# Down projection of the second block's FFN: the first group of hidden rows is loaded by token halves, between two weight blocks, and staged in tiles of its own

## The chip, the cores and the metric

The kernel runs on one core of a Trainium2 chip. The metric is the device time of one execution in microseconds (us). The trace was taken by the hardware profiler from one execution; the engines in it are TensorE (PE), VectorE (DVE), ScalarE (ACT), GpSimd (POOL) and SyncE (SP, which here only issues DMAs).

## The reference, cut to what matters

Two blocks run one after the other on 1024 tokens of width 1024. Each has two layers. The change is in the second half of each layer of the second block, a gated FFN with a short causal convolution; D_FF is 2816, which is 22 rows of 128.

```python
def conv_ffn(h, w_up, conv_w, conv_b, w_down):
    up = h @ w_up
    s_len = up.shape[1]
    padded = jnp.pad(up, ((0, 0), (CONV_WIDTH_2 - 1, 0), (0, 0)))
    conv = conv_b + padded[:, 0:s_len] * conv_w[0]
    for j in range(1, CONV_WIDTH_2):
        conv = conv + padded[:, j:j + s_len] * conv_w[j]
    gate, val = jnp.split(conv, 2, axis=-1)
    return (jax.nn.silu(gate) * val) @ w_down

def second_block(...):
    for l in range(DEPTH):
        ...
        x = x + conv_ffn(rms_norm(x, norm2_g[l]), w_up[l], conv_w[l], conv_b[l], w_down[l])
    return rms_norm(x, final_g)
```

## The kernel before

Every product is made of three matmuls on numbers that are split into a high and a low part (`mm3`): hi times hi (L226), lo times hi (L227) and hi times lo (L228), 128x128 by 128x512 each. So each operand is first split: ACT casts it to the high part (L214 for weights, L1358 for activations), and DVE subtracts that from the raw values (L201, in `split_lo`; in the FFN's up products one in six goes to POOL, L199).

`ffn` works in two parts. First come the 22 hidden rows. For each row `q` TensorE makes seven half-size products (`p12`, `p65`, `p7`, `p43`, a Strassen-like scheme), DVE adds them up (L1490, L1497, L1505 to L1507, L1512, L1515), `conv` runs the convolution (ACT L1463, then DVE L1465 twice for each side), `hidden` gates it (ACT L346, DVE L347, DVE L1471), and SP stores the row to DRAM (L1472, `hid_d`). Each row's tiles are two y tiles, `cv` and `fth`.

Then comes the down product. The 22 rows go through it in five groups, `[(0, 4), (4, 9), (9, 13), (13, 18), (18, 22)]`. `load_h(gi, j)` loads row `j` back, both token halves (`key` 0 and 1, 128x512 each, 256 KB), and splits them. `down(gi, m, ...)` loads weight block `m` of the group (`load_w`, L213) and makes the products of both halves; the first group's products are added to the residual, which is loaded for it (L1573, L1574), and the later groups' are added to that sum (L1570). After block `m >= 2` (`DS`) of a group one row of the next group is loaded.

All these loads, of hidden rows and of weights alike, land in the pool `wr`, which has three 256 KB buffers (tiles named `wraw`); a buffer is free again when ACT's cast and DVE's subtraction have read it. The split weights are in `wt` (four blocks), the split rows in the pools `left` (groups 0 to 3) and `dz` (group 4 alone, 16 tiles for hi and 16 for lo). `dz` takes its room from tiles of the FFN's activations and weights, so its first use waits for products that read those.

A scheduler orders the instructions of each engine from the order in the code, the buffers and its estimates of when each can run. Each engine and SP's queue then work through their own list strictly in order: where an instruction waits, all behind it on that list wait too.

Of the kernel before, what the change touches and what calls it, by code (L numbers as in the profile page):

```python
# [9 lines left out]
F32 = mybir.dt.float32  # L10
# [31 lines left out]
DS = 2  # L42
# [23 lines left out]
def run(steps):  # L66
    for _ in steps:
        pass
# [21 lines left out]
class Net:  # L90
# [1323 lines left out]
    def ffn(self, l, B, xd, finish):  # L1414

        nc, tc, I = self.nc, self.tc, self.I
        NJ = 22
        self.lo_pool = LP_FFN
        with self.right(f"fw{l}", 2) as fw, self.right(f"fe{l}", 2) as fe, self.right(f"ft{l}", 2) as ft:
# [3 lines left out]
            o, b = COLS["cw"][0] + 132 * l + 66, COLS["cb"][0] + 44 * l + 22  # L1423
# [52 lines left out]
            def mul(*ab):  # L1476

                ps = self.bank(self.all_banks)
                for i, ((hi, lo), b) in enumerate(ab):
                    for k in range(4):  # L1480
                        c = slice(k * 128, k * 128 + 128)
                        self.mm3(ps, hi[:, c], lo[:, c], B[b][k][0], B[b][k][1], i == 0 and k == 0, i == len(ab) - 1 and k == 3)
                return ps
# [36 lines left out]
            for q in range(HEAD):  # L1520
                (a11, a12), (a21, a22) = [[tuple(x[:, o:o + 512] for x in self.pre[2 * q + i]) for o in (0, 512)]
                                          for i in range(2)]
                ps = mul((a11, "11")), mul((a12, "21")), mul((a21, "11")), mul((a22, "21"))
# [17 lines left out]
        groups = [(0, 4), (4, 9), (9, 13), (13, 18), (18, 22)]  # L1541
        with ExitStack() as es:
            left = [es.enter_context(tc.tile_pool(name=f"hd{l}{i}", bufs=16 + 4 * i, reuse_waits="tile")) for i in range(2)]
            es3 = ExitStack()
            es3.enter_context(self.norm_scratch(f"f{l}"))
            xp, dz = [es3.enter_context(self.right(f"{n}{l}", 16)) for n in ("fx", "hz")]
            X = [[None] * 8 for key in range(2)]
            hid = {}

            def load_h(gi, j):  # L1550
                pool = dz if gi == 4 else left[gi % 2]
                for key in range(2):
                    raw = self.wr.tile([128, 512], F32, name="wraw", tag="wraw")
                    nc.sync.dma_start(out=raw, in_=self.hid_d[j, :, key * 512:key * 512 + 512])
                    hid[j, key] = self.split(pool, raw)

            def down(gi, m, keys, then):
                a, b = groups[gi]
                self.gemm_fm(I["w_down"][l, m][:, a:b], [(key, [hid[j, key] for j in range(a, b)], 512) for key in keys],
                             then, nk=b - a)  # L1560

            for j in range(*groups[0]):
                load_h(0, j)
            self.banks = self.all_banks
            for gi in range(4):
                nxt = list(range(*groups[gi + 1]))
                for m in range(8):
                    def ev(key, ps, n, gi=gi, m=m):
                        if gi:
                            nc.vector.tensor_add(X[key][m], ps, X[key][m])  # L1570
                            return
                        x = X[key][m] = xp.tile([128, 512], F32, name="fxn")
                        nc.sync.dma_start(out=x, in_=xd[m, :, key * 512:key * 512 + 512])  # L1573
                        nc.vector.tensor_add(x, ps, x)  # L1574

                    down(gi, m, [0, 1], ev)
                    if nxt and m >= DS:
                        load_h(gi + 1, nxt.pop(0))
            es.close()
            self.open_h(False)  # L1580
            self.banks = [(self.psA, "mm")]
            acc = [self.nm.tile([128, 512], F32, name="nacc", bufs=2) for key in range(2)]

            def last(key, m):
                def ev(key, ps, n):
                    x = X[key][m]
                    nc.vector.tensor_add(x, ps, x)
                    if l == 0:
                        nc.sync.dma_start(out=xd[m, :, key * 512:key * 512 + 512], in_=x)
                    self.sq_acc(acc[key], x, 512, m)  # L1590

                down(4, m, [key], ev)

            for m in range(8):
                last(0, m)
            self.meanwhile = lambda: [last(1, m) for m in range(MW)]
            norm = finish(0, X[0], acc[0])
            next(norm)
            for m in range(MW, 8):
                last(1, m)  # L1600
                for _ in range(NS):
                    next(norm, None)
            run(norm)
            run(finish(1, X[1], acc[1]))
            es3.close()
# [238 lines left out]
```

## Time and profile before

| | us |
|---|---|
| median of 3 runs | 3561.25 |
| lowest and highest of them | 3557.47, 3565.32 |
| the profiled execution's own time | 3559.54 |
| its span in the trace (first to last instruction) | 3557.5 |

The profiled execution has 2.0 us outside its span, and lies 1.7 us under the median. Of the span PE is busy 3420.8 us (96%), DVE 2479.8 (70%), ACT 1210.2 (34%) and POOL 628.3 (18%); the mean granted clock of TensorE is 0.984 of its full speed. The busy shares are averages over unlike stages, and what a stage is worth is read from the stage itself.

### The profile page before, as it was taken

How to read it: one execution, taken by the hardware profiler on the slowest of the kernel's cores; microseconds unless marked ns; L12 is line 12 of the kernel's file. 1: busy time of each engine (PE TensorE's matmuls, PEld its weight loads, DVE VectorE, ACT ScalarE, POOL GpSimd, SP SyncE). 2: the span in 40 equal slices, each digit the busy share in tenths (PEclk: the TensorE clock that was granted, in tenths of full speed). 3: DMA queues.
4: the chain of work that ended last, by engine and by line, in shares of the span. 5: the costliest groups of instructions: out<-in, count | busy, mean ns of one | idle time of the engine just before them, and what ended most of it. 6: DMA issues, size and time to landing. Idle time of an engine off the chain costs nothing.

```text
span 3557.5 us, 46933 instructions
## 1 busy us (share of the span) xinstructions
PE 3420.8 (96%) x17414; PEld 2725.9 (77%) x17414; DVE 2479.8 (70%) x3933; ACT 1210.2 (34%) x2189; POOL 628.3 (18%) x548
## 2 busy tenths in 40 slices
PE   7999999999989999999999998999999999999998
PEld 4888766788866687877788887887887878877786
DVE  5986578568467866454799998447355599999645
ACT  4115156331333641123344333223113243333322
POOL 4012321001033220220222320000030032222000
PEclk9999999999998999999999999999999999999999
DMA  6322365533223234316222224324324422222532
GB/s 204 87 78 83 104 183 167 174 107 97 75 87 94 82 125 140 92 46 192 78 86 83 77 80 136 117 87 150 86 60 132 144 80 77 77 78 69 174 100 92
DMA packets 245972, 380.70 MB, mean 107 GB/s; under 512 B 29104, under 2 KB 103792, under 8 KB 245232
## 3 DMA queue, kind: packets, MB, share of 16 engines
q1 hardware_dynamic: 237872, 370.37, 33.4%
q10 hardware_dynamic: 7872, 7.35, 0.8%
q8 instruction: 137, 2.24, 0.3%
q14 instruction: 91, 0.75, 0.1%
HBM read 280.35 MB, written 97.26 MB: 106 GB/s over the span
## 4 chain that ended last, share of the span: by engine, by line
PE 72%; DVE 14%; issue 5%; DMA 4%; ACT 3%; POOL 2%; SPq 0%; DVEq 0%; POOLq 0%; ACTq 0%
PE mm L226 13%; PE mm L227 13%; PE mm L228 13%; PE sc L226 4%; PE ax L226 4%; PE ax L227 3%; PE ax L228 3%; PE sc L227 3%; PE sc L228 3%; DVE wlo L201 2%; PE mm L956 2%; PE mm L942 2%; DVE cv L1465 1%; PE ax L715 1%; PE ax L1296 1%
## 5 line engine op out<-in xcount | busy, mean ns | idle before, releaser
L226 PE MATMUL mm<-hi,whi 128*128 128x512 f32 (+1 forms) x1780 | 690.8, 388 | 26.0 <-ACT whi L214 14.8
L228 PE MATMUL mm<-hi,wlo 128*128 128x512 f32 (+1 forms) x1780 | 685.9, 386 | 6.0 <-DVE wlo L201 6.0
L227 PE MATMUL mm<-lo,whi 128*128 128x512 f32 (+1 forms) x1780 | 688.0, 387 | 1.4 <-DVE lo L1651 1.1
L214 ACT CAST whi<-wraw 128x512 fp32r<-128x512 f32 (+3 forms) x412 | 232.3, 583 | 579.2 <-PE mm L227 247.8
L226 PEld LDWEIGHTS mm<-hi,whi 128*128 128x128 f32 x1780 | 337.5, 190 | 99.0 <-ACT whi L214 16.1
L228 PEld LDWEIGHTS mm<-hi,wlo 128*128 128x128 f32 x1780 | 336.8, 189 | 80.4 <-DVE wlo L201 9.4
L227 PEld LDWEIGHTS mm<-lo,whi 128*128 128x128 f32 x1780 | 337.5, 190 | 71.5 <-DVE lo L1651 3.1
L201 DVE TENSOR_TENSOR wlo<-wraw,whi 128x512 fp32r<-128x512 f32 (+3 forms) x412 | 269.4, 671 | 155.9 <-ACT whi L214 154.8
L226 PE MATMUL sc<-hi,whi 128*128 128x512 f32 x732 | 289.4, 395 | 12.5 <-ACT whi L214 10.6
L227 PE MATMUL sc<-lo,whi 128*128 128x512 f32 x732 | 288.2, 394 | 3.3 <-DVE lo L1651 3.3
L228 PE MATMUL sc<-hi,wlo 128*128 128x512 f32 x732 | 287.7, 393 | 1.6 <-DVE wlo L201 1.6
L226 PE MATMUL mm<-whi,hi 128*128 128x512 f32 (+2 forms) x704 | 259.5, 370 | 8.3 <-DVE ggt L347 8.3
L228 PE MATMUL mm<-whi,lo 128*128 128x512 f32 (+2 forms) x704 | 255.9, 364 | 0.0
L227 PE MATMUL mm<-wlo,hi 128*128 128x512 f32 (+2 forms) x704 | 255.6, 364 | 0.0
L188 POOL TENSOR_TENSOR rs<-rs,mhalf 128x4 f32<-128x4 f32 (+1 forms) x19 | 19.5, 1028 | 1072.3 <-DVE rs L183 1072.3
L498 DVE SCALAR_TENSOR_TENSOR ca<-u,wh,ca 128x1024 f32<-128x1024 f32 (+1 forms) x180 | 185.5, 1031 | 3.0
L226 PE MATMUL ax<-hi,whi 128*128 128x512 f32 x456 | 181.1, 397 | 4.8 <-DVE xn L1380 4.7
L228 PE MATMUL ax<-hi,wlo 128*128 128x512 f32 x456 | 179.8, 394 | 0.4 <-DVE wlo L201 0.4
L227 PE MATMUL ax<-lo,whi 128*128 128x512 f32 x456 | 179.9, 395 | 0.0
L201 DVE TENSOR_TENSOR wlo<-wr,whi 128x512 fp32r<-128x512 f32 x200 | 174.8, 885 | 0.0
L226 PEld LDWEIGHTS sc<-hi,whi 128*128 128x128 f32 x732 | 138.4, 189 | 43.8 <-ACT whi L214 11.2
L227 PEld LDWEIGHTS sc<-lo,whi 128*128 128x128 f32 x732 | 138.4, 189 | 35.5 <-DVE lo L1651 5.5
(367 smaller groups left out, 6568.7 us busy)
## 6 DMA issues: line engine op xcount, KB each, us to landing
wr<-in_w_up SPq DMA_DIRECT2D x80, 512.0 KB, 3.6
wraw<-in_w_fm SPq DMA_DIRECT2D x108, 256.0 KB, 3.1
wm<-in_w_mod SPq DMA_DIRECT2D x96, 256.0 KB, 3.8
wraw<-in_w_down SPq DMA_DIRECT2D x96, 256.0 KB, 2.8
hid_d<-fth SPq DMA_DIRECT2D x44, 512.0 KB, 2.6
wraw<-hid_d SPq DMA_DIRECT2D x88, 256.0 KB, 2.9
wraw<-in_w_out SPq DMA_DIRECT2D x80, 256.0 KB, 3.5
yl<-y_d SPq DMA_DIRECT2D x64, 256.0 KB, 3.3
```

What stands on the lines that cost most here:

```text
L188: nc.gpsimd.tensor_tensor(out, out, e, op=ALU.pow)
L201: nc.vector.tensor_sub(out, x, f(hi))
L214: nc.scalar.copy(hi[:, c], r)
L226: nc.tensor.matmul(ps, sh, mh, start=start, stop=False)
L227: nc.tensor.matmul(ps, sh, ml, start=False, stop=False)
L228: self.mark = nc.tensor.matmul(ps, sl, mh, start=False, stop=stop)
L498: self.not_before(nc.vector.scalar_tensor_tensor(a, u[:, j:j + n], wh[:, c, j:j + 1], a, op0=ALU.mult, op1=ALU.add))
L715: nc.tensor.matmul(o_, a_, b_, start=first_, stop=last_)
L942: nc.tensor.transpose(pt[:, j * 128:j * 128 + 128], P[:, h, kt * 128:kt * 128 + 128], self.ident)
L956: nc.tensor.matmul(po[half[u], :256], vst[:, vt, 64 * v:64 * v + 64], PT[kt][:, u * 256:u * 256 + 256], start=kt == 0, stop=kt == nkt - 1)
L1296: nc.tensor.matmul(pi[:, hv], A[h % 2][:, h // 2, :], V[:, j, hv], start=True, stop=True)
L1465: nc.vector.scalar_tensor_tensor(t[:, o:], x[:, 0:S - o], wc(2 - o), t[:, o:], op0=ALU.mult, op1=ALU.add)
```

## The change

The first group's eight half rows no longer go through `wr`: they are loaded into tiles of their own, named `hraw`, in `dz`, the place of the last group. The code's order is now: the four rows' first token half, weight block 0, the four rows' second half, weight block 1, and then all products of the group by `gemm_seq` with a lag of one, so that the second half of a weight block is multiplied one block later. Groups 1 to 3 are as before. Lines after the first group stand 16 lines lower in the changed kernel (the hidden loads are L1556 there, the residual's L1579).

```diff
--- before.py
+++ after.py
@@ -1547,10 +1547,12 @@
             X = [[None] * 8 for key in range(2)]
             hid = {}
 
-            def load_h(gi, j):
+            def load_h(gi, j, keys=(0, 1)):
                 pool = dz if gi == 4 else left[gi % 2]
-                for key in range(2):
-                    raw = self.wr.tile([128, 512], F32, name="wraw", tag="wraw")
+                for key in keys:
+
+                    raw = (self.wr.tile([128, 512], F32, name="wraw", tag="wraw") if gi else
+                           dz.tile([128, 512], F32, name="hraw", tag="h"))
                     nc.sync.dma_start(out=raw, in_=self.hid_d[j, :, key * 512:key * 512 + 512])
                     hid[j, key] = self.split(pool, raw)
 
@@ -1559,19 +1561,33 @@
                 self.gemm_fm(I["w_down"][l, m][:, a:b], [(key, [hid[j, key] for j in range(a, b)], 512) for key in keys],
                              then, nk=b - a)
 
-            for j in range(*groups[0]):
-                load_h(0, j)
+
+            a, b = groups[0]
+            wd = [I["w_down"][l, m][:, a:b] for m in range(8)]
+            early = []
+            for key in range(2):
+                for j in range(a, b):
+                    load_h(0, j, [key])
+                early.append(self.load_w(wd[key].rearrange("p k c -> p (k c)"), (b - a) * 128))
             self.banks = self.all_banks
-            for gi in range(4):
+            acts = [(key, [hid[j, key] for j in range(a, b)], 512) for key in range(2)]
+            nxt = list(range(*groups[1]))
+
+            def first_ev(m):
+                def ev(key, ps, n):
+                    x = X[key][m] = xp.tile([128, 512], F32, name="fxn")
+                    nc.sync.dma_start(out=x, in_=xd[m, :, key * 512:key * 512 + 512])
+                    nc.vector.tensor_add(x, ps, x)
+                    if key and nxt and m >= DS:
+                        load_h(1, nxt.pop(0))
+                return ev
+
+            self.gemm_seq([(wd[m], acts, first_ev(m)) for m in range(8)], 1, b - a, early)
+            for gi in range(1, 4):
                 nxt = list(range(*groups[gi + 1]))
                 for m in range(8):
-                    def ev(key, ps, n, gi=gi, m=m):
-                        if gi:
-                            nc.vector.tensor_add(X[key][m], ps, X[key][m])
-                            return
-                        x = X[key][m] = xp.tile([128, 512], F32, name="fxn")
-                        nc.sync.dma_start(out=x, in_=xd[m, :, key * 512:key * 512 + 512])
-                        nc.vector.tensor_add(x, ps, x)
+                    def ev(key, ps, n, m=m):
+                        nc.vector.tensor_add(X[key][m], ps, X[key][m])
 
                     down(gi, m, [0, 1], ev)
                     if nxt and m >= DS:
```

What the scheduler makes of it is alike in both layers; the rows below are of layer 0. In them `fth_19595` is hidden row 20, the last but one, and `fth_19740` row 21, the last.

On SP's queue, at the end of the hidden rows, before the change: the store of row 20, then half rows of group 0 (`wraw_19798` to `wraw_19810`), then the weight blocks 0 to 2, then row 4, the first row of group 1 (`wraw_19930`, `wraw_19936`). Three half rows of group 0 were loaded at the beginning of the FFN, two more stand just ahead of this piece.

```order
L1472 DMA hid_d_114<-fth_19595 128x1024
L1554 DMA wraw_19798<-hid_d_114 128x512
L1554 DMA wraw_19804<-hid_d_114 128x512
L1554 DMA wraw_19810<-hid_d_114 128x512
L213 DMA wraw_19818<-in_w_down 128x512
L213 DMA wraw_19856<-in_w_down 128x512
L213 DMA wraw_19894<-in_w_down 128x512
L1554 DMA wraw_19930<-hid_d_114 128x512
L1554 DMA wraw_19936<-hid_d_114 128x512
```

On SP's queue at the same place, after the change: `wraw_19952` to `wraw_20052` are row 4, row 5 and half of row 6 (all of group 1), `wraw_19966` and `wraw_20016` are the weight blocks 4 and 5, and the eight `hraw` are group 0, of which three are shown.

```order
L1472 DMA hid_d_114<-fth_19595 128x1024
L1556 DMA wraw_19952<-hid_d_114 128x512
L1556 DMA wraw_19958<-hid_d_114 128x512
L213 DMA wraw_19966<-in_w_down 128x512
L1556 DMA wraw_20002<-hid_d_114 128x512
L1556 DMA wraw_20008<-hid_d_114 128x512
L213 DMA wraw_20016<-in_w_down 128x512
L1472 DMA hid_d_114<-fth_19740 128x1024
L1556 DMA wraw_20052<-hid_d_114 128x512
L1556 DMA hraw_19768<-hid_d_114 128x512
L1556 DMA hraw_19774<-hid_d_114 128x512
L1556 DMA hraw_19780<-hid_d_114 128x512
```

The loads of group 1, two weight blocks and the store of the last row now stand ahead of the loads of group 0. Weight blocks 0 to 2 moved to the beginning of the FFN, where three half rows of group 0 were; block 3 stands just ahead of this piece.

On DVE, the last hidden row's end before the change (`cv_19714` and `cv_19736` are its two sides, `wlo` the weight blocks 0 to 2, `lo_19933` and `lo_19939` row 4 of group 1); the low parts of group 0 all stand ahead of this piece.

```order
L1465 SCALAR_TENSOR_TENSOR cv_19714<-y1_19683,ch_16596,cv_19714 128x1023
L1515 TENSOR_TENSOR y0_19615<-sc_19722,y0_19615 128x512
L1465 SCALAR_TENSOR_TENSOR cv_19714<-y1_19683,ch_16596,cv_19714 128x1022
L201 TENSOR_TENSOR wlo_19817<-wraw_19818,whi_19816 128x512
L1465 SCALAR_TENSOR_TENSOR cv_19736<-y0_19615,cols_82,cv_19736 128x1023
L201 TENSOR_TENSOR wlo_19855<-wraw_19856,whi_19854 128x512
L1465 SCALAR_TENSOR_TENSOR cv_19736<-y0_19615,cols_82,cv_19736 128x1022
L201 TENSOR_TENSOR wlo_19893<-wraw_19894,whi_19892 128x512
L201 TENSOR_TENSOR lo_19933<-wraw_19930,hi_19932 128x512
L347 SCALAR_TENSOR_TENSOR fth_19740<-fth_19740,cv_19736 128x1024
L201 TENSOR_TENSOR lo_19939<-wraw_19936,hi_19938 128x512
L1471 TENSOR_TENSOR fth_19740<-fth_19740,cv_19714 128x1024
```

On DVE the same place after the change, from the low part of the first `wraw` of group 1 on.

```order
L201 TENSOR_TENSOR lo_19955<-wraw_19952,hi_19954 128x512
L1465 SCALAR_TENSOR_TENSOR cv_19736<-y0_19615,cols_82,cv_19736 128x1022
L201 TENSOR_TENSOR lo_19961<-wraw_19958,hi_19960 128x512
L347 SCALAR_TENSOR_TENSOR fth_19740<-fth_19740,cv_19736 128x1024
L201 TENSOR_TENSOR lo_20005<-wraw_20002,hi_20004 128x512
L1471 TENSOR_TENSOR fth_19740<-fth_19740,cv_19714 128x1024
L201 TENSOR_TENSOR lo_20011<-wraw_20008,hi_20010 128x512
L201 TENSOR_TENSOR lo_20055<-wraw_20052,hi_20054 128x512
L201 TENSOR_TENSOR lo_19771<-hraw_19768,hi_19770 128x512
L201 TENSOR_TENSOR lo_19777<-hraw_19774,hi_19776 128x512
```

The low parts of rows 4, 5 and 6 (`lo_19955` to `lo_20055`) are interleaved with the last row's end, and the low parts of group 0 come behind it. ACT's casts stand in the same order as these low parts. On PE the first product of group 0 (`mm_19828`) takes `hi_19770`, the high part of `hraw_19768`, first.

## Rows read from the trace of the kernel before

**Rows 1.** PE's waits, 2060 to 2420 us (layer 0) and 3281 to 3490 us (layer 1); total, times, longest.

```profile
PE mm L226 <- ACT whi L214: 10.1, 1, 10.1
...
PE sc L226 <- ACT whi L214: 10.6, 1, 10.6
```

**Rows 2.** Chain that ended last, layer 0, around PE's wait; start us, us, what.

```profile
2180.07 0.70 DVE lo L201
2180.78 3.79 DMA wraw<-hid_d
...
2185.30 0.70 DVE lo L201
2186.02 2.65 DMA wraw<-in_w_down
...
2188.69 0.63 ACT whi L214
...
2189.36 0.80 PE mm L226
```

**Rows 3.** PE's timeline after each wait; start us, us, line, operation, idle before.

```profile
2194.90 0.39 PE L226 MATMUL mm<-hi,whi 128*128 128x512 f32 x1
...
3296.64 0.80 PE L226 MATMUL sc<-hi,whi 128*128 128x512 f32 x1 [10.58 <-ACT whi L214]
...
3300.63 0.39 PE L227 MATMUL sc<-lo,whi 128*128 128x512 f32 x1
```

**Rows 4.** Windows: us; PE, PEld, DVE, ACT, POOL busy; PEclk; DMA share; GB/s.

```profile
2120.00:2160.00 40.00, 40.00 (x174) 32.37 (x173) 38.23 (x43) 15.35 (x22) 10.11 (x6) 1.00 0.16 53
2189.40:2194.60 5.20, 5.20 (x12) 4.11 (x13) 4.73 (x7) 2.38 (x3) 0.00 (x0) 0.50 0.31 95
```

**Rows 5.** DVE's timeline, layer 0, end of the hidden rows.

```profile
2163.85 0.68 DVE L1497 TENSOR_TENSOR y<-mm,y 128x512 f32<-128x512 f32 x1
...
2167.76 0.69 DVE L1512 TENSOR_TENSOR y<-sc,y 128x512 f32<-128x512 f32 x1
...
2169.82 1.28 DVE L1465 SCALAR_TENSOR_TENSOR cv<-y,ch,cv 128x1023 f32<-128x1023 f32 x1 [0.78 <-ACT cv L1463]
...
2173.42 2.60 DVE L1465 SCALAR_TENSOR_TENSOR cv<-y,cols,cv 128x1023 f32<-128x1023 f32 x2
2175.93 0.68 DVE L1490 TENSOR_TENSOR y<-sc,y 128x512 f32<-128x512 f32 x1
...
2177.19 1.23 DVE L347 SCALAR_TENSOR_TENSOR fth<-fth,cv 128x1024 f32<-128x1024 f32 x1
2178.33 0.69 DVE L201 TENSOR_TENSOR lo<-wraw,hi 128x512 fp32r<-128x512 f32 x1
2178.93 1.22 DVE L1471 TENSOR_TENSOR fth<-fth,cv 128x1024 f32<-128x1024 f32 x1
...
2194.53 1.28 DVE L1465 SCALAR_TENSOR_TENSOR cv<-y,cols,cv 128x1022 f32<-128x1022 f32 x1
...
2197.19 1.23 DVE L347 SCALAR_TENSOR_TENSOR fth<-fth,cv 128x1024 f32<-128x1024 f32 x1 [0.18 <-ACT fth L346]
```

**Rows 6.** DVE's timeline, layer 1, the last but one row's end.

```profile
3281.30 0.68 DVE L1490 TENSOR_TENSOR y<-ax,y 128x512 f32<-128x512 f32 x1
3282.56 1.23 DVE L347 SCALAR_TENSOR_TENSOR fth<-fth,cv 128x1024 f32<-128x1024 f32 x1 [0.58 <-ACT fth L346]
```

**Rows 7.** SP's timeline in the FFN of layer 0; start us, us of issuing.

```profile
1788.24 0.38 SPq L1472 DMA_DIRECT2D hid_d<-fth  x1
1793.51 0.33 SPq L1554 DMA_DIRECT2D wraw<-hid_d  x1
1793.93 0.89 SPq L1442 DMA_DIRECT2D wr<-in_w_up  x1
...
2203.46 6.43 SPq L1573 DMA_DIRECT2D fxn<-x_d  x10
```

**Rows 8.** All hidden loads (L1554) of the kernel, from issue to landing.

```profile
DMA to landing us min/median/max: 2.4/2.9/6.1
```

## The prediction

> **What bounds the kernel now.** I read the list of PE's waits around the down products first, since PE is busy 96% of the span and only a wait of PE is worth anything. It has one line in each layer [rows 1]: PE stands still for 10.1 us in layer 0 and 10.6 us in layer 1, between the last product of the hidden rows and the first down product, and waits for nothing else in that stretch. So the change can win the 20.7 us of these two waits and what hangs on them, and no more; the lag of one, which is to spare later products a wait, finds none there to spare.
>
> The chain shows what makes up the wait [rows 2]. A DVE low part frees a `wr` buffer at about 2180.7, a hidden load goes out in it and takes 3.79 us, its low part frees the buffer again, weight block 0 goes out, lands after 2.65 us, is cast, and PE starts at 2189.36. Two loads stand one behind the other through three buffers, and the buffers are freed by DVE. DVE in turn is late: it is busy 38.23 of 40 us in the FFN [rows 4] and still has the last row's L347 to do at 2197.19 [rows 5], when PE has been out of hidden rows since 2189.36 - 10.1 = 2179.3. So at this place DVE is some 18 us behind PE, and whatever waits for DVE's last instructions comes late.
>
> The wait has a second price. After it the granted clock is 0.50 for a while [rows 4], which is 1.2 GHz where 1.00 is 2.4: from 2189.36 to 2194.90 in layer 0, and from 3296.64 to 3300.63 in layer 1 [rows 2, 3]. Of these 5.5 and 4.0 us about half is lost, 4.8 us in all.
>
> **What the change does to the restart.** Had the staged loads gone out as soon as their place was free, they would stand clear of the buffers. But in SP's order after the change five loads of group 1, weight blocks 4 and 5, and the store of row 21 stand ahead of them. The last, `wraw_20052`, needs the third buffer back from `lo_20011`, and on DVE `lo_20011` stands behind the last row's L1471. Before, group 0's loads needed nothing of the last row's L347 and L1471; now they stand behind both.
>
> That a wait in SP's queue holds what stands behind it is seen in the trace [rows 7]. A store went out at 1788.24, nothing for 5.3 us, then a hidden load at 1793.51, and 0.42 us behind it a load of up weights, which goes into a pool of its own. The Trainium skill, "DMA: Bandwidth & Descriptors", section "Anatomy of one DMA — SWDGE (gpsimd) path", says that any wait for a semaphore happens on the issuing sequencer, before dispatch. By that rule the staged loads wait with the group 1 load ahead of them, and the time is that of the sum below; without it they could pass, as in the rival on the other side. The row agrees, for SP's queue.
>
> **The restart in layer 0, worked out.** I start from row 21's L1490, at 2175.93 [rows 5], up to which DVE's order is the same but for which raw values a low part is taken of, and walk DVE's new order to the start of `lo_20011`. Each step is the distance of starts in a row of the same instructions:
> L1490 and a low part 1.26 (to 2177.19), row 20's L347 1.14 (to 2178.33), and L1471, of the same size, 1.14: 3.54.
> L1497 to L1512: 3.91 for the row before, which had two low parts between; now one, so less 0.60 (a low part, 2178.33 to 2178.93): 3.31.
> L1512 to L1465, with ACT's L1463 between: 2.06. From there to side 0's first L1465, one low part included: 3.60.
> That L1465, half of the 2.51 us that two take, 1.25, and `lo_19955` 0.60: 1.85.
> The second L1465 to L347, with a low part and ACT's tanh between: 2.66.
> L347 1.14, `lo_20005` 0.60, L1471 1.14: 2.88.
> The sum is 19.90, so `lo_20011` starts at 2195.83. The loads that these low parts need keep up just so: `lo_20005` stands 4.40 us behind the start of `lo_19955`, which frees its buffer, and the cycle is 0.71 to the issue, 2.9 to land [rows 8] and 0.63 of cast [rows 2], 4.24.
>
> From there: 0.71 from the low part's start to the load that takes its buffer (2180.07 to 2180.78), 0.64 to the next issue (10 loads in 6.43 us) [rows 7], 3.79 to land, 0.67 from cast to PE [rows 2]. PE starts at 2201.64 in place of 2189.36: **12.3 us later**. For the landing I take 3.79 and not the median 2.9 [rows 8], because that load, as the new one, goes out just behind a store of 512 KB.
>
> **Layer 1.** Row 21's L1490 starts at 3281.30 and L347 1.26 later [rows 6]. Here a low part stands between L347 and L1471, so the first step is 1.26 + 1.14 + 0.60 + 1.14 = 4.14, the sum 20.50, and the low part that stands where `lo_20011` does in layer 0 starts at 3301.80. With 5.81 behind it PE starts at 3307.61 and not 3296.64 [rows 3]: **11.0 us later**.
>
> **The rest of the edits, at nothing.** Weight blocks 0 to 2 are loaded at the FFN's beginning, in buffers that then held hidden rows; the loads, casts and low parts are as many as before. The staged tiles' place was last read by products that PE has long done. After the restart PE needs a new half row for each three matmuls: 3 x 0.43 = 1.3 us at the half clock (12 in 5.20) and 3 x 0.23 = 0.69 at full clock (174 in 40 us) [rows 4], and they go out 0.64 apart, so they keep up; if not, it costs under 1 us a layer. Weight block 4 is cast behind the eight half rows, 8 x 0.63 = 5 us, while PE has eight products or 96 x 0.23 = 22 us to do with the four blocks at hand. The half clock after the wait I leave as long as it was; the longer wait could change that, and as no row shows a wait of 22 us here I bound it by none and by twice what it is, 4.8 us either way.
>
> **Sum.** 12.28 + 10.97 = 23.2 us on the profiled execution's 3559.54 (a span of 3557.5 and 2.0 outside) gives 3582.8. The median of the runs shown is 1.7 higher, so 3584.5.
>
> Bounds: a landing of 2.4 or 6.1 in place of 3.79 [rows 8] gives -2.8 or +4.6 for both layers. If DVE's idle times in the walk (0.78 and 0.18, and 0.58 more in layer 1) [rows 5, 6] all vanished, -2.5. With the clock's 4.8 either way that is 3574 to 3594.
>
> **Rivals.** *The staged loads are not held* (faster). They go out when their place is free, before PE has run out, and both waits nearly vanish, with the half clock behind them: at most 20.7 + 4.8 = 25.5, less about 1 us a wait, so about 3538. For it speaks that these tiles need no buffer of `wr`; against it SP's order and [rows 7], and beyond that DVE's order, in which the low part of the first staged row, which PE's second matmul needs, also stands behind the last row's L1471. It decides where `lo_20011` starts before 2189.36 - 5.81 = 2183.5 in layer 0, 12.3 us of a walk of 19.9 earlier. Chance 0.07.
> *The restart comes when it did* (no change). The staged loads end about when the old weight load ended, because DVE is less late than the walk says. The eight low parts that no longer stand in the tail, 8 x 0.60 = 4.8 us, speak for it, but the walk leaves them out already, and it has only about 1 us of idle time in layer 0. 3561. Chance 0.06.
> *Half the loss* (slower by less). DVE catches up some 4 to 7 us a layer, for instance because ACT's tanh and convolution start come sooner with fewer casts ahead: 3567 to 3574, about 3570. Chance 0.08.
> *A longer loss.* The `wr` loads ahead land late, up to 6.1 us [rows 8]; then the cycle of 4.24 becomes 7.4, past the 4.40 that DVE leaves it, and moves `lo_20011` by up to 3 us a layer, on top of the bound above: 3589 + 6 = 3595. Chance 0.06.
>
> **How the numbers follow.** The forecast has 0.73; with the smaller and the longer loss, 0.87 lie on the slower side. A measurement of this kernel can tell about 0.2%, 7 us, from no change: faster 0.07, same 0.06, slower 0.87. The range reaches from 3570, the middle of the smaller loss, to 3595, the middle of the longer one: it leaves out the first two rivals (0.13) and about half of the other two (0.07), which is 2 in 10.
>
> **What would show it.** In the changed profile PE's wait before group 0 should be 22.4 us and 21.6 us, ended by ACT's cast of an `hraw`; the first staged load should go out near 2197.2 and 3303.2, 0.6 us behind a load of a `wraw` that waited for a DVE low part, itself right behind L1471. The later groups should show no new wait. Wrong it would be if the staged loads go out ahead of that low part, if DVE reaches L1471 of row 21 before 2190, or if the wait is longer but the half clock behind it is gone.

## The result, and the profile after

The changed kernel takes 3585.98 us in the median of 4 runs (3582.16 to 3589.82), against 3563.28 us for the kernel before in 4 runs (3557.47 to 3566.28). The ratio is 1.0068 with a 95% interval of 1.0047 to 1.0089: slower by 22.7 us, where 23.2 were forecast. The profiled execution took 3582.16 us (span 3580.4), 22.6 more than that of before.

PE's waits of the changed kernel, 2060 to 2420 us and 3281 to 3520 us, answer to [rows 1]; the columns are the total, the times and the longest. The other lines of the first list lie before the down products.

```profile
PE mm L226 <- ACT hi L1358: 22.5, 1, 22.5
...
PE sc L226 <- ACT hi L1358: 21.5, 1, 21.5
```

Each layer still has one wait, no longer ended by the cast of weight block 0 but by that of a hidden half row. It was 10.1 and 10.6 us.

SP's timeline of the changed kernel at that place shows what the half rows wait for; start, us of issuing.

```profile
2181.28 0.32 SPq L1472 DMA_DIRECT2D hid_d<-fth  x1
2182.48 3.64 SPq L1556 DMA_DIRECT2D wraw<-hid_d  x2
2190.25 0.33 SPq L213 DMA_DIRECT2D wraw<-in_w_down  x1
2192.09 2.07 SPq L1556 DMA_DIRECT2D wraw<-hid_d  x2
2196.24 0.33 SPq L213 DMA_DIRECT2D wraw<-in_w_down  x1
2197.38 0.32 SPq L1472 DMA_DIRECT2D hid_d<-fth  x1
2197.98 0.32 SPq L1556 DMA_DIRECT2D wraw<-hid_d  x1
2198.35 4.31 SPq L1556 DMA_DIRECT2D hraw<-hid_d  x8
```

PE has run out at 2203.26 - 22.47 = 2180.79. The queue gets through nine entries in the 17 us from 2181.28 on, each when DVE has freed a buffer or ended a row, and all eight staged loads follow without a gap, 0.37 us behind the last `wraw`. They show no wait of their own, so what held them was the queue's order. Whether their place held them too is taken up with the third run.

DVE's timeline of the changed kernel, the walk of the prediction from L1490 to the low part that frees the last buffer; it answers to [rows 5].

```profile
2177.50 0.69 DVE L1490 TENSOR_TENSOR y<-sc,y 128x512 f32<-128x512 f32 x1
...
2194.39 1.23 DVE L347 SCALAR_TENSOR_TENSOR fth<-fth,cv 128x1024 f32<-128x1024 f32 x1 [0.57 <-ACT fth L346]
2195.53 0.68 DVE L201 TENSOR_TENSOR lo<-wraw,hi 128x512 fp32r<-128x512 f32 x1
2196.13 1.22 DVE L1471 TENSOR_TENSOR fth<-fth,cv 128x1024 f32<-128x1024 f32 x1
2197.27 0.68 DVE L201 TENSOR_TENSOR lo<-wraw,hi 128x512 fp32r<-128x512 f32 x1
2202.57 0.69 DVE L201 TENSOR_TENSOR lo<-wraw,hi 128x512 fp32r<-128x512 f32 x1 [4.62 <-ACT hi L1358]
```

From 2177.50 to 2197.27 are 19.77 us, against the 19.90 of the walk. After it DVE itself has nothing to do for 4.6 us: with the last row done, all wait for the load.

PE's timeline of the changed kernel at the two restarts; it answers to [rows 3].

```profile
2203.26 0.80 PE L226 MATMUL mm<-hi,whi 128*128 128x512 f32 x1 [22.47 <-ACT hi L1358]
...
2206.57 0.39 PE L227 MATMUL mm<-lo,whi 128*128 128x512 f32 x1
...
3319.10 0.80 PE L226 MATMUL sc<-hi,whi 128*128 128x512 f32 x1 [21.54 <-ACT hi L1358]
...
3322.55 0.40 PE L227 MATMUL sc<-lo,whi 128*128 128x512 f32 x1
```

The matmuls are back at 0.39 to 0.40 us after 3.3 and 3.4 us, where it took 5.5 and 4.0 before. The full clock comes back a little sooner after the longer wait, worth some 1 us in layer 0.

### The profile page after: what moved, and what is told of

Same layout as the page of the kernel before. It is cut to its first block, busy times and chain, and to the rows that moved or that the text cites. A ratio compares the mean times of both kernels' runs of the same rounds, so it can differ in the third digit from the quotient of the medians.

```text
span 3580.4 us, 46898 instructions
## 1 busy us (share of the span) xinstructions
PE 3416.6 (95%) x17414; PEld 2720.5 (76%) x17414; DVE 2487.1 (69%) x3933; ACT 1209.2 (34%) x2189; POOL 630.9 (18%) x548
## 5 line engine op out<-in xcount | busy, mean ns | idle before, releaser
L188 POOL TENSOR_TENSOR rs<-rs,mhalf 128x4 f32<-128x4 f32 (+1 forms) x19 | 19.6, 1029 | 1090.5 <-DVE rs L183 1090.5
L228 PEld LDWEIGHTS sc<-hi,wlo 128*128 128x128 f32 x732 | 137.8, 188 | 36.8 <-DVE wlo L201 6.8
```

The source lines that it names most:

```text
L188: nc.gpsimd.tensor_tensor(out, out, e, op=ALU.pow)
L228: self.mark = nc.tensor.matmul(ps, sl, mh, start=False, stop=stop)
```

## The experiments

Every comparison is with the kernel before, run beside it on the same chip. The runs were made in three batches on three chips, so runs of unlike batches, and the change itself, are compared by these ratios. The theory was that the staged loads are held in SP's queue by entries that wait for the last hidden row's end on DVE. Rivals were the order (halves, lag, one product after the other), and the landing of eight loads at once.

**First: the staging alone.** To the kernel before:

```diff
-                    raw = self.wr.tile([128, 512], F32, name="wraw", tag="wraw")
+                    raw = (self.wr.tile([128, 512], F32, name="wraw", tag="wraw") if gi else
+                           dz.tile([128, 512], F32, name="hraw", tag="h"))
```

> The kernel before with one part of the change: the first group's eight half rows go into tiles of their own in the last group's place; row by row, weights behind them, no lag, as before. Theory (held loads: the staged loads stand in SP's queue behind loads and a store that wait for the last hidden row's end on DVE): the loss is all here. SP's order again has rows of group 1, weight blocks and the store of row 21 ahead of the staged loads, with one more low part on DVE ahead of the last of them; PE waits 22 to 26 us in each layer, the time is 22 to 32 us above before. Rival (order: the loss comes from halves, lag, and products made one after the other): within 5 us of before, PE's waits 10 to 12 us.

Measured: 3587.58 us, ratio 1.0074 (1.0056 to 1.0093), 26 us slower. Its waits of PE:

```profile
PE mm L226 <- ACT hi L1358: 24.1, 1, 24.1
...
PE sc L226 <- ACT hi L1358: 23.8, 2, 23.1
```

The staging alone brings the whole loss. The rival of the order falls.

**Second: the order without the staging.** To the changed kernel:

```diff
-                    raw = (self.wr.tile([128, 512], F32, name="wraw", tag="wraw") if gi else
-                           dz.tile([128, 512], F32, name="hraw", tag="h"))
+                    raw = self.wr.tile([128, 512], F32, name="wraw", tag="wraw")
```

> The changed kernel with its order (first halves, weight block 0, second halves, block 1, lag of one) but without the staging: the first group's half rows go through the three wr buffers again. Theory (held loads): no loss; weight block 0 goes out at about 2179 in layer 0 and not 2186, PE starts some 7 us sooner than before, then waits some 3 us for block 1; in all 0 to 8 us faster than before. Rival (order): about as slow as the change, 15 to 25 us above before. Rival (landing: eight loads at once come late): no loss either, but no earlier start than before.

Measured: 3554.13 us, ratio 0.9983 (0.9966 to 1.0000), some 6 us faster than before, at the edge of what the interval can tell. PE's waits from 2174 to 2420 us in layer 0, which stand in the place of the 10.1 us of [rows 1], and SP's queue:

```profile
PE mm L226 <- ACT whi L214: 3.2, 1, 3.2
PE ax L226 <- ACT whi L214: 2.9, 1, 2.9
```

```profile
2176.11 0.33 SPq L213 DMA_DIRECT2D wraw<-in_w_down  x1
2177.25 0.32 SPq L1472 DMA_DIRECT2D hid_d<-fth  x1
2177.85 5.74 SPq L1555 DMA_DIRECT2D wraw<-hid_d  x4
2183.93 6.89 SPq L213 DMA_DIRECT2D wraw<-in_w_down  x3
```

Weight block 0 goes out ahead of row 20's store at 2176.11, where PE runs out at 2179.48 - 3.20 = 2176.28; before it went out at 2186.02 [rows 2], 6.8 us after PE had run out. So the loss and a small gain were in one change, and the three buffers that the staging was to get round are not what holds the loads most.

**Third: the staged loads ahead of group 1.** To the changed kernel, a dependency for the scheduler alone on each load of group 1 (the diff is cut: `ld` is the load, and `behind` puts it after the last staged load in the scheduler's order):

```diff
+                    if gi == 0:
+                        self.staged = ld
+                    elif gi == 1:
+                        self.behind(ld)
```

> The changed kernel with the scheduler told that the loads of group 1's rows stand behind the last staged load; no wait is added. The staged loads then stand right behind the store of row 21, which needs L1471. If the loads of group 1 ahead of them were the whole cause (rival), PE starts no later than before and the time is that of before within 7 us. By the walk of the prediction only two low parts and one load less stand ahead: L1471 ends near 2194.5, the first staged load goes out near 2195.2 and not 2198.3, PE's waits are about 19.5 us in each layer, the time 16 to 20 us above before.

Measured: 3577.42 us, ratio 1.0052 (1.0034 to 1.0070), 16 to 19 us slower by medians and ratio; waits of 20.0 and 20.3 us. SP's queue and the two rows of DVE that end row 20 and row 21 (line numbers are 6 higher here):

```profile
2177.68 15.45 SPq L1478 DMA_DIRECT2D hid_d<-fth  x2
2193.22 4.18 SPq L1562 DMA_DIRECT2D hraw<-hid_d  x8
```

```profile
2176.42 1.23 DVE L1477 TENSOR_TENSOR fth<-fth,cv 128x1024 f32<-128x1024 f32 x1
...
2191.56 1.23 DVE L1477 TENSOR_TENSOR fth<-fth,cv 128x1024 f32<-128x1024 f32 x1
```

The two stores are one entry each, 15 us apart, and the staged loads go out right behind the second. The loads of group 1 ahead of them cost only about 2 us a layer; the store of row 21, and with it DVE's last instruction of the hidden rows, holds them as well. The rival that group 1's loads are the whole cause falls. So does another, that the staged tiles' place came free late: the first staged load goes out 16.0 us after PE has run out here, 17.6 with the change and 19.9 in the first run, each time 0.4 us behind the entry ahead of it.

**Fourth: a place that comes free sooner.** As the third, and

```diff
-                           dz.tile([128, 512], F32, name="hraw", tag="h"))
+                           left[1].tile([128, 512], F32, name="hraw", tag="h"))
```

> The kernel of the run before, with the staged tiles in the place of group 1's split rows, which comes free before PE runs out of hidden rows. SP's order then has the staged loads behind the store of row 20 and ahead of that of row 21. Theory (held loads, then the next thing held): the staged loads go out near 2180 in layer 0, but ACT casts them behind the last row's L1463 at about 2188, and DVE has their low parts between L1465, L347 and L1471 up to 2196, so PE starts at about 2189 to 2190 and stutters until then; the time is 0 to 10 us above before, 13 to 23 us under the change. Rival (landing): the loads land as late as with the change after their issue, 4 us, and the time stays within 5 us of the change.

Measured: 3558.30 us, ratio 0.9994 (0.9983 to 1.0005), no difference from before and by the ratios some 26 us under the change, a little more than the 13 to 23 expected. Its longest PE waits are 9.5 and 8.5 us. SP, ACT and DVE in layer 0:

```profile
2185.13 0.32 SPq L1478 DMA_DIRECT2D hid_d<-fth  x1
2185.54 4.35 SPq L1562 DMA_DIRECT2D hraw<-hid_d  x8
```

```profile
2192.31 1.24 ACT L1469 ACTIVATE cv<-y,cols 128x1024 f32<-128x1024 f32 x1 [1.45 <-DVE y L1521]
2193.46 1.64 ACT L1364 CAST hi<-hraw 128x512 fp32r<-128x512 f32 x3
```

```profile
2181.36 0.69 DVE L1496 TENSOR_TENSOR y<-sc,y 128x512 f32<-128x512 f32 x1
```

Now the store of row 20 is the last thing ahead of them, and with the loads in time the next engine holds: ACT casts them behind the last row's `conv`, which waits for DVE. The times lie some 5 us later than expected since this execution, the longest of the ten, reaches L1490 (L1496 here) at 2181.36 and not 2175.93. Landing as the cause falls: the eight loads of a layer took as long to land here, 4.0 to 6.7 us against 4.2 to 6.7 with the change, and cost nothing.

**Fifth: the second without the lag.**

```diff
-            self.gemm_seq([(wd[m], acts, first_ev(m)) for m in range(8)], 1, b - a, early)
+            self.gemm_seq([(wd[m], acts, first_ev(m)) for m in range(8)], 0, b - a, early)
```

> The second run's kernel (halves through wr, weight block 0 between them) with a lag of 0 and not 1: block 0 is multiplied with both halves before block 1. If the gain of the second run comes from where weight block 0 stands in SP's queue (theory), this keeps it: PE starts after a wait of about 3 to 5 us, the second half of block 0 then stutters until its last low part (near 2190 in layer 0), and the time is within 4 us of the second run, 3 to 11 us under before. If the gain comes from the lag (rival), it is lost: within 3 us of before or slower.

Measured: 3554.71 us, ratio 0.9990 (0.9977 to 1.0002). Against the second run's ratio that is 2.5 us, less than the intervals. The first wait is again 3.2 us in layer 0, so it is weight block 0's place in the queue that shortened it; what the lag is worth, between nothing and a few us, stays open.

**Sixth and seventh: two and three weight blocks ahead of the second halves**, through `wr` (the seventh with `(0, 1, 2)` and a lag of 2):

```diff
-                early.append(self.load_w(wd[key].rearrange("p k c -> p (k c)"), (b - a) * 128))
+                for i in ((0, 1), ())[key]:
+                    early.append(self.load_w(wd[i].rearrange("p k c -> p (k c)"), (b - a) * 128))
```

> The second run's kernel with weight block 1 loaded ahead of the second halves and not behind them. Theory (what PE needs next must stand ahead in the queue): the second wait of 2.7 to 2.9 us, for block 1, is gone in both layers, since the block goes out just behind the store of row 20 and lands near 2182; the half clock behind the waits ends sooner; 2 to 9 us faster than the second run, about 3547. Rival (the lateness of DVE comes back through the second halves' low parts, which now stand later): the waits move to L227 or L226 of the second halves and the time stays within 2 us of the second run.

> As the run before, with three weight blocks ahead of the second halves and a lag of two, so PE has three products of the first halves before it needs a second half. If the second halves' low parts were the next wait, this hides them: a few us faster than the run before. If they were not, the third block only takes a buffer from the second halves: within 3 us of it.

Measured: 3555.42 us, ratio 0.9984 (0.9973 to 0.9995), and 3554.26 us, ratio 0.9978 (0.9967 to 0.9989). My expectation for the sixth was wrong, its rival right: the wait for block 1 is gone, but the low parts of the second halves, from DVE, take its place in layer 0. Waits of the sixth from 2176 to 2420 us:

```profile
PE sc L227 <- DVE lo L201: 3.5, 2, 2.7
PE mm L226 <- ACT whi L214: 3.1, 1, 3.1
```

The third block hides part of that (1.7 us left); its gain over the sixth is inside the intervals.

**Eighth: the first halves on POOL.** The changed kernel with the staged tiles in `left[1]`, and for `key` 0 of group 0 loads by `nc.gpsimd.dma_start`, cast and subtraction on GpSimd.

> The changed kernel with the staged tiles in group 1's place, and the first halves' four loads issued from POOL's queue and cast and split by POOL, which is idle there; so they wait for no store, no wr buffer, and neither ACT nor DVE. The second halves go as in the change. Theory (held by SP's queue and by what ACT and DVE still have to do): the first staged loads go out by about 2178 in layer 0, when PE has not run out yet, and the wait of 22 us shrinks to less than 6; POOL's pace, some 3 us for a half row, and the second halves, split on DVE behind L1471, make new waits, so that the time is between 5 us under and 8 us above before. Rival (the place comes free late, or the loads land late): the first staged load goes out or is split no sooner than in the fourth run, near 2190.

Measured: 3559.84 us, ratio 0.9996 (0.9987 to 1.0005). POOL's timeline and PE's waits in layer 0:

```profile
2163.51 0.77 POOL L1556 DMA_DIRECT2D hraw<-hid_d  x1 [2.88 <-PE mm L227]
2175.88 0.56 POOL L1556 DMA_DIRECT2D hraw<-hid_d  x1 [11.59 <-PE sc L227]
2176.78 1.08 POOL L1556 DMA_DIRECT2D hraw<-hid_d  x2 [0.35 <-PE sc L228]
2177.86 1.05 POOL L1561 CAST hi<-hraw 128x512 fp32r<-128x512 f32 x1
```

```profile
PE mm L227 <- POOL lo L1562: 4.0, 4, 1.4
PE mm L226 <- POOL hi L1561: 2.8, 2, 2.5
PE sc L227 <- DVE lo L201: 1.5, 4, 0.8
```

On POOL's queue nothing ahead waits for DVE, and the first staged load goes out 13 us before PE runs out at 2178.96 - 2.48 = 2176.48. But these loads wait for PE, which frees their places: the other three go out at 2175.88 and later. POOL's casts stand behind them, so it begins to split only 1.4 us after PE has run out, 14 us after the first load went out. Here POOL's own order holds what SP's held before. The wait of 22 us becomes ten of at most 2.5, 8.3 us in all, a little more than the 6 I expected. POOL takes 0.6 to 2.1 us for each step. The waits of both layers, 8.3 and 7.0 us, are 5.4 less than before, and still the kernel is no faster that can be told.

**Ninth and tenth: weight block 0 ahead of the first halves** in the seventh's kernel, and that with the second halves' low parts on POOL (`self.lo_pool = 6` around their loads; the diff shows the ninth):

```diff
+                for i in ((0,), (1, 2))[key]:
+                    early.append(self.load_w(wd[i].rearrange("p k c -> p (k c)"), (b - a) * 128))
                 for j in range(a, b):
                     load_h(0, j, [key])
-                for i in ((0, 1, 2), ())[key]:
-                    early.append(self.load_w(wd[i].rearrange("p k c -> p (k c)"), (b - a) * 128))
```

> The seventh run's kernel (three weight blocks ahead of the second halves, lag of two, all through wr) with weight block 0 ahead of the first halves, so that it is loaded and split early in the FFN. Theory: the first wait, 3.2 and 4.7 us for the cast of block 0, goes, since PE can begin with rows 0 and 1, and a shorter one for rows 2 and 3 takes its place; 3 to 8 us faster than the seventh run if the half clock behind the wait shortens too, at least 1 us if it does not. Rival (what is lost behind the wait is the half clock, not the wait, and any gap brings it): within 3 us of the seventh run.

> The run before with the low parts of the four second halves on POOL, which is idle there, and not on DVE. Theory (DVE's lateness is what the second halves wait for): DVE ends the last row 2.4 us sooner and PE's waits for these low parts vanish; 0 to 5 us faster than the run before. Rival (POOL takes 1.3 to 1.8 us for a low part and DVE 0.60): the waits only move to POOL, no gain.

Measured: 3555.40 us, ratio 0.9989 (0.9977 to 1.0001), and 3555.32 us, ratio 0.9983 (0.9972 to 0.9994). The ninth misses the gain that I expected, and the tenth adds nothing that can be told. The two longest lines in the list of the ninth's waits in layer 0:

```profile
PE mm L227 <- DVE lo L201: 3.2, 5, 0.8
PE mm L228 <- DVE wlo L201: 2.4, 1, 2.4
```

The waits of 3.2 and 4.7 us for block 0 are gone, as expected, and none is over 2.4 us. But they are many: both layers sum to 12.0 us, where the seventh has 11.5, and the clock falls all the same (below). Of all ten the seventh has the lowest ratio, 0.9978, but the intervals of all six runs through `wr` overlap. These six lie 0.10 to 0.22% under the kernel before, four of them with an interval that ends at or below it, and by the ratios 0.8 to 0.9% under the change.

**The waits of all runs together.** Over both layers PE waits 20.7 us at this place before. Where the waits grow, the time follows: 44.0 with the change, 47.9 in the first run and 40.3 in the third are 23.3, 27.2 and 19.6 us more, and the ratios give 24, 26 and 19. Where they shrink, less of it shows: 18.2 in the fourth run and 13.7, 13.2, 13.9, 11.5, 15.3, 12.0 and 9.8 in the second and the fifth to the tenth are 3 to 11 us less, and the ratios give 1 to 8.

## Why the prediction was right

The forecast held, and so did its main steps. That 22.7 us were measured where 23.2 were forecast is partly luck: the interval of the ratio reaches from 17 to 32 us. What bears the forecast out are the two waits and the order on the queues.

- *One wait a layer is all there is to win or lose.* After the restart there is again no wait in the down products, and the two waits grew by 22.47 - 10.12 = 12.35 and 21.54 - 10.58 = 10.96 us; 12.28 and 10.97 were forecast.
- *The place in SP's queue decides.* Shown by the first run (staging alone: all of the loss), the second (no staging: none), the third (without group 1's loads ahead they go out right behind the last row's store) and the fourth (ahead of that store: no loss). In the eighth both queue and place are others, so it says less. The Trainium skill, "DMA: Bandwidth & Descriptors", section "Anatomy of one DMA — SWDGE (gpsimd) path", puts any semaphore wait of a DMA on the issuing sequencer, before dispatch. The row 2198.35 agrees: eight loads without a wait of their own, out at once behind one that had one. So does POOL in the eighth run, which sat idle for 11.59 us at its second load.
- *The walk on DVE.* 19.77 us against 19.90; in layer 1 from L1490 at 3292.82 to the low part at 3313.15, 20.33 against 20.50. It worked because the steps were distances of starts in the same sequence, waits for ACT included. One step was misread: the 2.66 us from the second L1465 to L347 come from a stretch with two low parts, not one. From 2191.93 to 2194.39 it took 2.46 us, ended by ACT's tanh as before, so the error was small.
- *From the low part to PE.* 2203.26 - 2197.27 = 5.99 us against 5.81. Two errors partly cancelled: the staged loads follow the `wraw` by 0.37 us, not 0.64, and PE starts 4.91 us after the first one's issue, where 3.79 + 0.67 = 4.46 were put. The term that was too small is the landing; all sixteen staged loads:

```profile
DMA to landing us min/median/max: 4.2/5.6/6.7
```

- *The half clock left as it was.* It became shorter by about 1 us in layer 0; the bound of 4.8 was wide.
- *The other edits at nothing.* Right for the changed kernel within the noise, but not by themselves: without the staging the order of halves and weights is worth some 6 us, since block 0 no longer stands behind the second halves. I had looked for a gain only in the waits behind the restart, where there is none, and not in which load stands ahead of the first product. In the change the staging hid it: by ratios, +0.74% for the staging alone, -0.17% for the order alone, +0.68% together.

One rival was added up wrongly: 4 to 7 us a layer off the forecast of 3584.5 is 3570 to 3576, not 3567 to 3574. With it the range's lower end, 3570, would lie some 3 us higher, still far from the 3586 measured.

That this execution's hidden rows end 1.5 us later (PE runs out at 2180.79 and not 2179.24) was not in the sum; the clock's 1 us and other small differences take most of it back.

## What to carry to other kernels

A load that gets a buffer of its own is not free of the old buffers: it still stands in its queue, and in the order of the engines that split it, and a scheduler may put waiting loads ahead of it. The place itself moves that order: in the fourth run another place was all that differed from the third, and the staged loads went ahead of the last row's store. Look at what stands ahead of the first thing that the critical engine needs next, and at what the last entry there waits for; here that was an engine 16 us behind. Before giving a transfer more room, try giving it an earlier place: the same loads through the same three buffers, with the first weight block sooner, took some 6 us less than before and 30 less than the change (second run, by the ratios).

## What the runs showed of the hardware that was not expected

How long TensorE stays at the half clock did not follow how long it had stood. After the 22.47 us wait it was back in 3.3 us, after 10.12 us in 5.5; in layer 1 after 21.54 us in 3.4, after 10.58 us in 4.0. And short gaps bring it too: in the ninth run, with no wait over 2.4 us, these windows (us; busy time of PE, PEld, DVE, ACT, POOL; granted clock; DMA share; GB/s) show

```profile
2176.00:2180.00 4.00, 3.26 (x13) 1.99 (x11) 3.61 (x6) 1.08 (x2) 0.00 (x0) 1.00 0.73 227
2180.00:2184.00 4.00, 2.16 (x6) 0.99 (x7) 3.27 (x5) 0.77 (x2) 0.00 (x0) 1.00 0.70 228
2184.00:2188.00 4.00, 4.00 (x11) 3.12 (x11) 1.89 (x3) 1.90 (x3) 0.00 (x0) 0.57 0.32 94
2188.00:2192.00 4.00, 3.62 (x16) 2.63 (x14) 3.48 (x4) 2.56 (x4) 0.00 (x0) 1.00 0.32 103
```

The clock falls to 0.57 behind a stretch in which PE was busy 2.16 of 4 us, while it is itself busy all the time: 11 matmuls in 4 us where full speed makes 17. So part of what a shorter wait gives comes back as half clock. Products that start 0.43 us apart, not 0.23, number some 20 in the two layers before, 10 with the change and just under 40 in the second run and in the ninth; by these counts about 3 us of what the second run saves go back, which is an estimate. The half clock does not set the ninth behind the second: it is alike in both, and so are the sums of the waits, 12.0 and 13.7 us.
